# Sparse 3x3 convolution on one core: all input loads issued at the start, the first store held until the seventh load has landed

## The chip, the cores and the metric

The kernel runs on one core of one Trainium2 chip. The metric is the device time of one execution in microseconds (us), as the median of several runs. One core has five engines that run side by side and meet at semaphores: TensorE (PE, matmuls), VectorE (DVE), ScalarE (ACT), GpSimd (POOL) and SyncE (SP, which here only issues transfers). Transfers between the main memory (HBM) and the on-chip memory (SBUF) are carried by 16 DMA engines, which both transfer queues of this kernel share: SP's queue (q1 in the profile) and POOL's queue (q0).

## The reference

```python
def setup_inputs():
    batch, c_in, h, w, c_out, k = 16, 64, 64, 64, 128, 3
    ...
def reference(x, weight):
    x_pad = np.pad(x, ((0, 0), (0, 0), (pad, pad), (pad, pad)), mode='constant')
    ...
                        if weight[co, ci, kh, kw] != 0:
                            output[b, co] += weight[co, ci, kh, kw] * x_pad[b, ci, kh:kh+h, kw:kw+w]
```

It is a 3x3 convolution with padding 1 over 16 images of 64 channels and 64x64 points, to 128 output channels, all in float32. Nine tenths of the weights are zero, but not in a pattern that the kernel uses. The input x is 16.8 MB, the weight 0.3 MB, the output 33.6 MB.

## The kernel before

**Tiling.** Two images are worked on together as a pair, so there are eight pairs. A pair's input lies in one SBUF tile `xs[p]` of 128 partitions (image of the pair and channel) by 64x64 points in bf16, 8 KB per partition. The output of a pair is one tile of 128 output channels by 2 images by 64x64 points in float32, 32 KB per partition.

**Loads.** POOL issues the loads of x (`load`, L67 and L68), and each converts float32 to bf16 on the way, so that a load reads 2 MB and writes 1 MB. Pair 0 is split: its lower 32 rows come by POOL (L63), its upper 32 rows come unconverted by SP into `x_head` (L62) and are cast by VectorE and ScalarE (`cast_x`, L101). SP also loads the weight (L60). Then POOL issues pairs 1 to 3 and the first 24 rows of pair 4 at once (L72 to L77). The rest of the input is issued from inside the loop over pairs, each load behind POOL's last sum of a pair: the rest of pair 4 in pair 1, pair 5 in pair 2, pair 6 in pair 3, and the halves of pair 7 in pairs 4 and 5 (L196 to L199).

**Work of a pair.** A pair is cut into four blocks of 16 rows. All but one go through `twos` (L166): POOL adds each even row and the odd row below it into `s` (L169); TensorE multiplies `s` with the middle row of taps, ScalarE copies this shared product from PSUM into `pc` (L176), TensorE computes the even and the odd rows with differences of taps, and VectorE adds `pc` to them into the output tile (L183). The first block of pair 0 goes through `direct` (L159) without sums. TensorE's instructions stand in program order.

**Stores.** When a pair is complete, SP stores its 4.2 MB in one transfer (L207), and the last pair in two halves (L205). The output tiles come from a pool of three buffers: pair 3 writes where pair 0's output lay, so it waits until that store has landed. After pair 1's store SP issues five transfers of one number each into `spare` (L209 to L211). Each transfer of a queue signals on one of eight semaphores in turn, so these five shift which semaphore the later stores use.

**Order.** The schedule is the program's order on each engine (`manual_schedule`); the framework adds the semaphore waits from the memory that instructions read and write.

Of the kernel before, what the change touches and what calls it, by code (L numbers as in the profile page):

```python
# [8 lines left out]
FP32 = mybir.dt.float32  # L9
BF16 = mybir.dt.bfloat16  # L10
# [17 lines left out]
def kernel(  # L28
# [6 lines left out]
    nc = tc.nc  # L35

    B, C_IN, H, W = x.shape
    C_OUT, _, KH, KW = weight.shape
    assert (B, C_IN, H, W) == (16, 64, 64, 64) and (C_OUT, KH, KW) == (128, 3, 3)
    NP = B // 2  # L40
    HEAD = 32

    const_pool = ctx.enter_context(tc.tile_pool(name="const", bufs=1))
    x_pool = ctx.enter_context(tc.tile_pool(name="x", bufs=1))
    s_pool = ctx.enter_context(tc.tile_pool(name="s", bufs=3))
    p_pool = ctx.enter_context(tc.tile_pool(name="pc", bufs=4))
    o_pool = ctx.enter_context(tc.tile_pool(name="o", bufs=3))
    psum_pool = ctx.enter_context(
        tc.tile_pool(name="psum", bufs=8, space=bass.MemoryType.PSUM)
    )  # L50
# [4 lines left out]
    def pair(p):  # L55
        return x[2 * p : 2 * p + 2].rearrange("n i h w -> (n i) h w")

    xs = [x_pool.tile([128, H, W], BF16, name=f"x{p}") for p in range(NP)]
    w_sb = const_pool.tile([C_OUT, C_IN * KH * KW], FP32, name="w_sb")
    nc.sync.dma_start(out=w_sb, in_=weight.rearrange("o i kh kw -> o (i kh kw)"))  # L60
    x_head = const_pool.tile([128, HEAD, W], FP32, name="x_head")
    nc.sync.dma_start(out=x_head, in_=pair(0)[:, 0:HEAD, :])  # L62
    nc.gpsimd.dma_start(out=xs[0][:, HEAD:H, :], in_=pair(0)[:, HEAD:H, :])  # L63
    ident = const_pool.tile([128, 128], BF16, name="ident")
    make_identity(nc, ident)

    def load(p, a=0, b=H):  # L67
        nc.gpsimd.dma_start(out=xs[p][:, a:b, :], in_=pair(p)[:, a:b, :])  # L68

    EARLY, CUT = 4, 24  # L72

    LATER = {2: (5,), 3: (6,), 4: (7, 0, 32), 5: (7, 32, 64)}
    for p in range(1, EARLY):
        load(p)
    load(EARLY, 0, CUT)  # L77


    idle_rhs = const_pool.tile([128, 512], BF16, name="idle_rhs")  # L80
# [78 lines left out]
    def direct(p, o, r0, rows):  # L159
        ps = product(  # L160
            [(xs[p], G1, r0, 1), (xs[p], G0, r0 - 1, 1), (xs[p], G2, r0 + 1, 1)], rows
        )
        nc.scalar.copy(out=o[0][:, r0 : r0 + rows, :], in_=ps[0])  # L163
        nc.vector.tensor_copy(out=o[1][:, r0 : r0 + rows, :], in_=ps[1])  # L164

    def twos(p, o, r0):  # L166
        t0 = r0 // 2
        s = s_pool.tile([128, 8, W], BF16, name="s")
        nc.gpsimd.tensor_tensor(  # L169
            out=s, in0=xs[p][:, r0 : r0 + 16 : 2, :], in1=xs[p][:, r0 + 1 : r0 + 16 : 2, :], op=ADD  # L170
        )
        shared = product([(s, G1, 0, 1)], 8)
        pc = []
        for n in range(2):
            c = p_pool.tile([128, 8, W], FP32, name="pc")
            nc.scalar.copy(out=c, in_=shared[n])  # L176
            pc.append(c)
        even = [(xs[p], G21, r0 + 1, 2), (xs[p], G0, r0 - 1, 2)]
        odd = [(xs[p], G01, r0, 2), (xs[p], G2, r0 + 2, 2)]
        for first, terms in ((r0, even), (r0 + 1, odd)):  # L180
            ps = product(terms, 8)
            for n in range(2):
                nc.vector.tensor_tensor(  # L183
                    out=o[n][:, first : r0 + 16 : 2, :], in0=ps[n], in1=pc[n], op=ADD
                )

    for p in range(NP):
        both = o_pool.tile([C_OUT, 2, H, W], FP32, name="o")
        o = [both[:, n] for n in range(2)]
        into = out[2 * p : 2 * p + 2].rearrange("n o h w -> o n h w")  # L190
        last = p == NP - 1
        for blk in range(4):
            r0 = 16 * blk
            if BLOCKS[p][blk] == "T":
                twos(p, o, r0)
                if p == 1 and blk == 3:  # L196
                    load(EARLY, CUT, H)
                elif blk == 3 and p in LATER:
                    load(*LATER[p])  # L199
            else:  # L200
                for r, rows in ((r0, 8), (r0 + 8, 8)):
                    direct(p, o, r, rows)
            if last and blk % 2 == 1:
                rows = slice(r0 - 16, r0 + 16)
                nc.sync.dma_start(out=into[:, :, rows, :], in_=both[:, :, rows, :])  # L205
        if not last:
            nc.sync.dma_start(out=into, in_=both)  # L207
        if p == 1:
            spare = const_pool.tile([1, 5], FP32, name="spare")  # L209
            for k in range(5):  # L210
                nc.sync.dma_start(out=spare[:, k : k + 1], in_=weight[0:1, 0, 0, 0:1])  # L211


# [28 lines left out]
```

## Time and profile before

| What | Value |
|---|---|
| Median of 3 runs | 126.06 us (125.84 to 131.06) |
| Profiled execution, span from first to last instruction | 124.3 us |
| PE busy | 108.7 us (87%) |
| DVE, ACT, POOL busy | 82.5, 39.0, 41.7 us |
| q1 (SP's transfers) | 34.90 MB, 67.2% of 16 engines' span |
| q0 (POOL's loads, bytes as they land) | 7.86 MB, 30.7% |
| Issue of pair stores on SP, first and last | 23.0 us, 99.8 us |
| Issue of the two halves of pair 7 | 106.2 us, 112.6 us |
| A 4.2 MB store, issue to landing (median) | 19.8 us |

The profile is one execution taken by the hardware profiler. Its span leaves out what lies before the first and after the last instruction, so the runs' times are somewhat longer than the span. A share of busy time is an average over the span. In the page's slices, a digit is the busy share of one fortieth of the span in tenths. The rate of the DMA engines counts bytes at their destination.

### The profile page before, as it was taken

Reading aid. Unit: us, or ns where it says so; the run is one execution under the profiler, and the core shown is the slowest. Engines: PE = TensorE matmul, PEld = TensorE weight load, DVE = VectorE, ACT = ScalarE, POOL = GpSimd, SP = SyncE. Lnnn points to the kernel's source line nnn. Section 1 sums busy time; section 2 is a strip of 40 time slices with the busy share of each in tenths; the row PEclk is TensorE's granted clock in tenths of the full one; section 3 lists DMA queues with packets and bytes.
Section 4 is the critical chain, followed back from the end, with each engine's and each line's share of the span. In section 5 each row is a group of like instructions: output and inputs, shape, how many; then the busy total and the mean of one; then the engine's idle time right before and its main releaser. Section 6 shows DMA issues by size and latency. Waiting matters only on the chain.

```text
span 124.3 us, 2453 instructions
## 1 busy us (share of the span) xinstructions
PE 108.7 (87%) x989; PEld 57.2 (46%) x989; DVE 82.5 (66%) x135; ACT 39.0 (31%) x71; POOL 41.7 (34%) x47
## 2 busy tenths in 40 slices
PE   6959999999999999999999999999999999970000
PEld 2425555555555555555555555555555555530000
DVE  0353577877787778777877878887877787772000
ACT  4543333333333333333333333333333333330000
POOL 6409333533353335333443335333333320000000
PEclk9999999999999999999999999999999999997555
DMA  4999999999999999999999999999999999999991
GB/s 120 348 220 227 219 213 213 238 411 338 335 392 422 319 316 324 377 340 329 303 385 378 354 380 443 376 349 389 418 422 437 422 427 427 437 427 403 432 414 82
DMA packets 4198, 42.91 MB, mean 345 GB/s; under 512 B 347, under 2 KB 347, under 8 KB 1115
## 3 DMA queue, kind: packets, MB, share of 16 engines
q1 hardware_dynamic: 2746, 34.90, 67.2%
q0 software_dynamic: 1440, 7.86, 30.7%
q8 instruction: 7, 0.11, 0.3%
q14 instruction: 5, 0.03, 0.1%
HBM read 17.07 MB, written 33.55 MB: 407 GB/s over the span
## 4 chain that ended last, share of the span: by engine, by line
PE 82%; DMA 5%; DVE 1%; issue 1%; DVEq 0%; SPq 0%
PE ps L150 82%; DMA x_head<-in_x_dram 5%; DVE o L183 1%; DVEq L237 0%; DVE x L101 0%; SPq L60 0%; DVEq L183 0%
## 5 line engine op out<-in xcount | busy, mean ns | idle before, releaser
L183 DVE TENSOR_TENSOR o<-ps,pc 128x512 f32<-128x512 f32 x124 | 77.8, 686 | 22.1 <-PE ps L150 19.2
L150 PE MATMUL ps<-x,wT 64*128 64x504 bf16 (+3 forms) x780 | 88.8, 373 | 1.3 <-DVE x L101 1.3
L150 PEld LDWEIGHTS <-wT 64*128 64x128 bf16 x966 | 55.2, 94 | 49.5 <-issue 1.7
L169 POOL TENSOR_TENSOR s<-x 128x512 bf16<-128x512 bf16 x31 | 35.6, 1150 | 57.6 <-PE ps L150 41.1
L176 ACT COPY pc<-ps 128x512 f32<-128x512 f32 x62 | 33.3, 589 | 64.0 <-issue 61.8
L150 PE MATMUL ps<-s,wT 64*128 64x512 bf16 (+1 forms) x186 | 25.7, 377 | 0.0
L86 PE MATMUL ps<-idle_rhs 128*128 128x512 bf16 x14 | 4.8, 505 | 1.2 <-DVE idle_rhs L81 1.2
L68 POOL DMA_DIRECT2D x<-in_x_dram x9 | 5.0, 560 | 0.0
L86 PEld LDWEIGHTS <-idle_rhs 128*128 128x128 bf16 x14 | 1.5, 118 | 3.2 <-issue 1.4
L105 DVE CAST w_bf<-w_sb 128x192 bf16<-128x192 f32 (+1 forms) x4 | 1.1, 351 | 2.5 <-DMA w_sb<-in_weight_dram 2.5
L164 DVE COPY o<-ps 128x512 f32<-128x512 f32 x2 | 1.4, 692 | 2.0 <-PE ps L150 2.0
L101 DVE CAST x<-x_head 128x576 bf16<-128x576 f32 x1 | 0.5, 460 | 2.6 <-DMA x_head<-in_x_dram 2.6
L101 ACT CAST x<-x_head 128x576 bf16<-128x576 f32 (+1 forms) x2 | 1.5, 802 | 1.8 <-DMA x_head<-in_x_dram 1.8
L163 ACT COPY o<-ps 128x512 f32<-128x512 f32 x2 | 1.2, 586 | 2.4 <-PE ps L150 2.4
L105 ACT ACT_TABLE_LOAD x1 | 1.3, 1283 | 0.7 <-PEq L226 0.7
L105 ACT CAST w_bf<-w_sb 128x64 bf16<-128x64 f32 (+1 forms) x2 | 0.7, 416 | 1.6 <-DMA w_sb<-in_weight_dram 1.6
L115 DVE TENSOR_TENSOR wT<-ps,wT 128x384 bf16<-128x384 f32 x2 | 1.0, 548 | 0.0
L111 PEld LDWEIGHTS <-w_bf 128*128 128x128 bf16 x9 | 0.5, 97 | 1.0 <-DVE w_bf L105 1.0
L63 POOL DMA_DIRECT2D x<-in_x_dram x1 | 0.7, 693 | 0.8 <-POOLq L226 0.8
L111 PE MATMUL ps<-ident,w_bf 128*128 128x128 bf16 x9 | 0.9, 222 | 0.1
L81 DVE MEMSET idle_rhs<- 128x256 uint32 x1 | 0.3, 272 | 0.9 <-PEq L226 0.9
L126 DVE CAST wT<-ps 128x384 bf16<-128x384 f32 x1 | 0.6, 551 | 0.0
(8 smaller groups left out, 1.9 us busy)
## 6 DMA issues: line engine op xcount, KB each, us to landing
out_dram<-o SPq DMA_DIRECT2D x7, 4096.0 KB, 19.8
x<-in_x_dram POOLq DMA_DIRECT2D x5, 1024.0 KB, 16.8
out_dram<-o SPq DMA_DIRECT2D x2, 2048.0 KB
x<-in_x_dram POOLq DMA_DIRECT2D x3, 512.0 KB, 13.8
x_head<-in_x_dram SPq DMA_DIRECT2D x1, 1024.0 KB, 6.2
x<-in_x_dram POOLq DMA_DIRECT2D x1, 640.0 KB, 14.8
x<-in_x_dram POOLq DMA_DIRECT2D x1, 384.0 KB, 22.3
w_sb<-in_weight_dram SPq DMA_DIRECT2D x1, 288.0 KB
```

Source lines behind the costliest of these rows:

```text
L68: nc.gpsimd.dma_start(out=xs[p][:, a:b, :], in_=pair(p)[:, a:b, :])
L86: nc.tensor.matmul(idle_ps, idle_rhs[:, 0:128], idle_rhs, start=True, stop=True)
L101: copy(out=xs[0][:, a:b, :], in_=x_head[:, a:b, :])
L105: copy(out=w_bf4[:, g, a:b, :], in_=w_v[:, k : k + b - a, :])
L111: nc.tensor.matmul(wps[:, j, :], src, ident, start=True, stop=True)
L115: nc.vector.tensor_tensor(out=wT[:, g], in0=wps, in1=wT[:, G1], op=SUB)
L150: nc.tensor.matmul(ps[n][:, lo:hi, c_lo:c_hi], tap(g, kw, n), src[q, a:b:step, c_lo + kw - 1 : c_hi + kw - 1], start=(i == 0), stop=(i == ...
L163: nc.scalar.copy(out=o[0][:, r0 : r0 + rows, :], in_=ps[0])
L164: nc.vector.tensor_copy(out=o[1][:, r0 : r0 + rows, :], in_=ps[1])
L169: nc.gpsimd.tensor_tensor(out=s, in0=xs[p][:, r0 : r0 + 16 : 2, :], in1=xs[p][:, r0 + 1 : r0 + 16 : 2, :], op=ADD)
L176: nc.scalar.copy(out=c, in_=shared[n])
L183: nc.vector.tensor_tensor(out=o[n][:, first : r0 + 16 : 2, :], in0=ps[n], in1=pc[n], op=ADD)
```

## The change

- All of pairs 1 to 7 are loaded by POOL in one run ahead of everything else (`UP_FRONT = 8`); the loads inside the loop, and the splits of pairs 4 and 7, are gone.
- SP's first store, that of pair 0, gets an added wait: it is issued only when the load of pair 6 (`GATE = 6`, the seventh pair) has landed.
- There are four output tiles instead of three, used in turn. The fourth is one piece of memory, `shared_home`, with `x_head` and the input tiles of pairs 0, 1 and 2: pairs 3 and 7 write their output there.
- The five tiny transfers move from behind pair 1's store to the start, behind the loads of the weight and of `x_head`.

```diff
-    o_pool = ctx.enter_context(tc.tile_pool(name="o", bufs=3))
...
-    xs = [x_pool.tile([128, H, W], BF16, name=f"x{p}") for p in range(NP)]
+    shared_home = const_pool.tile([128, 4, H * W // 2], FP32, name="home")
+    x_head = shared_home[:, 0, :].rearrange("c (h w) -> c h w", w=W)
+    xs = [
+        shared_home[:, 1 + p, :].bitcast(BF16).rearrange("c (h w) -> c h w", w=W)
+        for p in range(3)
+    ]
+    xs += [x_pool.tile([128, H, W], BF16, name=f"x{p}") for p in range(3, NP)]
+    outs = [const_pool.tile([C_OUT, 2, H, W], FP32, name=f"o{k}") for k in range(3)]
+    outs.append(shared_home.rearrange("o (n r) (h w) -> o n (r h) w", n=2, w=W))
...
-    EARLY, CUT = 4, 24
-
-    LATER = {2: (5,), 3: (6,), 4: (7, 0, 32), 5: (7, 32, 64)}
-    for p in range(1, EARLY):
-        load(p)
-    load(EARLY, 0, CUT)
+    UP_FRONT, GATE = 8, 6
+    landed = {p: load(p) for p in range(1, UP_FRONT)}
+    spare = const_pool.tile([1, 5], FP32, name="spare")
+    for k in range(5):
+        nc.sync.dma_start(out=spare[:, k : k + 1], in_=weight[0:1, 0, 0, 0:1])
...
-        both = o_pool.tile([C_OUT, 2, H, W], FP32, name="o")
+        both = outs[p % 4]
...
-                if p == 1 and blk == 3:
-                    load(EARLY, CUT, H)
-                elif blk == 3 and p in LATER:
-                    load(*LATER[p])
...
-        if not last:
-            nc.sync.dma_start(out=into, in_=both)
-        if p == 1:
-            spare = const_pool.tile([1, 5], FP32, name="spare")
-            for k in range(5):
-                nc.sync.dma_start(out=spare[:, k : k + 1], in_=weight[0:1, 0, 0, 0:1])
+        if not halves:
+            store = nc.sync.dma_start(out=into, in_=both)
+            if first:
+                tc.add_manual_dep(
+                    store.ins,
+                    landed[GATE].ins.name,
+                    mybir.DependencyInfo(
+                        mybir.DependencyClass.Sync, mybir.DependencyReason.DATA
+                    ),
+                    reason="stores begin when the loads are nearly through",
+                )
+                first = False
```

More of the change, by code (lines that the diff above doesn't have):

```diff
@@ L56, in pair @@
         return x[2 * p : 2 * p + 2].rearrange("n i h w -> (n i) h w")
-    xs = [x_pool.tile([128, H, W], BF16, name=f"x{p}") for p in range(NP)]
+    shared_home = const_pool.tile([128, 4, H * W // 2], FP32, name="home")
[7 more added lines that the diff above has]
+    outs.append(shared_home.rearrange("o (n r) (h w) -> o n (r h) w", n=2, w=W))
     w_sb = const_pool.tile([C_OUT, C_IN * KH * KW], FP32, name="w_sb")
     nc.sync.dma_start(out=w_sb, in_=weight.rearrange("o i kh kw -> o (i kh kw)"))
-    x_head = const_pool.tile([128, HEAD, W], FP32, name="x_head")
     nc.sync.dma_start(out=x_head, in_=pair(0)[:, 0:HEAD, :])
@@ L67, in load @@
     def load(p, a=0, b=H):
-        nc.gpsimd.dma_start(out=xs[p][:, a:b, :], in_=pair(p)[:, a:b, :])
-    EARLY, CUT = 4, 24
-    LATER = {2: (5,), 3: (6,), 4: (7, 0, 32), 5: (7, 32, 64)}
-    for p in range(1, EARLY):
-        load(p)
-    load(EARLY, 0, CUT)
+        return nc.gpsimd.dma_start(out=xs[p][:, a:b, :], in_=pair(p)[:, a:b, :])
+    UP_FRONT, GATE = 8, 6
[3 more added lines that the diff above has]
+        nc.sync.dma_start(out=spare[:, k : k + 1], in_=weight[0:1, 0, 0, 0:1])
     idle_rhs = const_pool.tile([128, 512], BF16, name="idle_rhs")
@@ L185, in twos @@
                 )
+    first = True
     for p in range(NP):
-        both = o_pool.tile([C_OUT, 2, H, W], FP32, name="o")
+        both = outs[p % 4]
         o = [both[:, n] for n in range(2)]
         into = out[2 * p : 2 * p + 2].rearrange("n o h w -> o n h w")
-        last = p == NP - 1
+        halves = p == NP - 1
         for blk in range(4):
@@ L202 @@
                     direct(p, o, r, rows)
-            if last and blk % 2 == 1:
+            if halves and blk % 2 == 1:
                 rows = slice(r0 - 16, r0 + 16)
                 nc.sync.dma_start(out=into[:, :, rows, :], in_=both[:, :, rows, :])
-        if not last:
-            nc.sync.dma_start(out=into, in_=both)
-        if p == 1:
-            spare = const_pool.tile([1, 5], FP32, name="spare")
-            for k in range(5):
-                nc.sync.dma_start(out=spare[:, k : k + 1], in_=weight[0:1, 0, 0, 0:1])
+        if not halves:
[10 more added lines that the diff above has]
+                first = False
 _INS = ['x', 'weight']
```

## Prediction

> **What bounds the kernel now.** I read the page's slices first, because engines and transfers stand side by side there.
>
> ```profile
> PE   6959999999999999999999999999999999970000
> DMA  4999999999999999999999999999999999999991
> GB/s 120 348 220 227 219 213 213 238 411 338 335 392 422 319 316 324 377 340 329 303 385 378 354 380 443 376 349 389 418 422 437 422 427 427 437 427 403 432 414 82
> ```
>
> Two rows are full. TensorE works from 7.95 us to about 111 and then stops; the DMA engines work from the second slice to the last. So the end is a matter of transfers, while TensorE sets when each store may start. The rate row looks as if the loads ran at half speed (220 against 430), but it counts the bytes that arrive: x is float32 in memory and bf16 when it lands, so a load moves two bytes for each byte counted. The views of the DMA queues over three stretches allow a fair count: loads alone, loads and stores mixed, stores alone.
>
> ```profile
> DMA packets 464, 3.22 MB, mean 215 GB/s; under 512 B 58, under 2 KB 58, under 8 KB 81
> q0 software_dynamic: 463, 3.21, 102.6%
> ...
> DMA packets 2103, 23.42 MB, mean 360 GB/s; under 512 B 174, under 2 KB 174, under 8 KB 668
> q1 hardware_dynamic: 1244, 19.17, 70.4%
> q0 software_dynamic: 851, 4.15, 31.1%
> ...
> DMA packets 1007, 12.82 MB, mean 427 GB/s; under 512 B 64, under 2 KB 64, under 8 KB 65
> q1 hardware_dynamic: 1003, 12.80, 100.2%
> ```
>
> The stretches are 8 to 23 us, 23 to 88 and 88 to 118. Counting loads (q0) double and adding 0.02 to 0.1 MB of instruction fetch, the rates are 6.44 MB / 15 us = 429 GB/s for loads alone, 27.57 MB / 65 us = 424 for the mixture, 12.83 MB / 30 us = 427.7 for stores alone. The mixture is slower by about one per cent and no more. The same count gives 8.78 MB before 23 us and 1.59 MB after 118, together 50.77 MB.
>
> The windows show how it ends (the last two numbers of a row are the share of 16 DMA engines and GB/s), and the timeline when SP issues the stores of pairs 0 and 1, the five tiny transfers, and the last two stores:
>
> ```profile
> 118.00:120.00 2.00, 0.00 (x0) 0.00 (x0) 0.00 (x0) 0.00 (x0) 0.00 (x0) 0.50 0.99 422
> 120.00:122.00 2.00, 0.00 (x0) 0.00 (x0) 0.00 (x0) 0.00 (x0) 0.00 (x0) 0.50 0.78 332
> 122.00:124.30 2.30, 0.00 (x0) 0.00 (x0) 0.00 (x0) 0.00 (x0) 0.00 (x0) 0.50 0.09 36
> ```
>
> ```profile
> 23.03 13.13 SPq L207 DMA_DIRECT2D out_dram<-o  x2
> 36.22 4.93 SPq L211 DMA_DIRECT2D spare<-in_weight_dram  x5
> 48.58 51.60 SPq L207 DMA_DIRECT2D out_dram<-o  x5
> 106.16 6.82 SPq L205 DMA_DIRECT2D out_dram<-o  x2
> ```
>
> The last store is issued at 112.6, and its 2.1 MB would take 4.9 us on a free queue; data ends near 123, so a backlog stood before it. The 16 engines do not stop together: some stop just before 121 us, the last at 123. The chain of waits ends at 112.6 and puts 82% on TensorE: it does not follow the last transfers, and I do not use it for the end.
>
> **The change, part by part.**
>
> *Bytes.* Eight loads instead of ten carry the same bytes; stores and weights are the same. Whatever the change gains in transfers, it gains by rate.
>
> *Order.* After 23 us the kernel before moves 27.57 MB mixed, in 65 us. Now the 8.30 MB of loads in it go alone: 8.30 / 0.429 = 19.35 us, to 42.35 us. The 19.17 MB of stores go alone at 427.7 GB/s, 44.8 us, and 0.1 MB of instruction fetch takes 0.25. Together 64.4 us against 65.0: a gain of 0.6 us. From below, if order is worth nothing, 0. From above, the largest rate of one slice (443) is one slice's scatter, so I do not take it; 433 for all mixed bytes, the best 5 us window of stores alone (95 to 100 us), would give 1.3 us.
>
> A rule speaks against this gain. The Trainium skill, page "HBM Reference", section "Specifications (TRN2)", says that a core streaming alone gets about 425 GB/s and is held by its 16 DMA engines. By that rule the order of reads and writes is worth nothing; 50.77 MB at 425 would be an estimated 119.5 us in either order. The 424 of the mixture agrees; that the two unmixed stretches stand 0.9 to 1.2% higher is what I set against it.
>
> *The wait of the first store.* Through pair 6 the loads have 8.30 - 2.10 = 6.20 MB left at 23 us: 14.45 us, to 37.5. A load lands later than its mean data, since the slowest engine decides: pair 3's, issued at 3.53, landed at 24.17, where the byte count puts its data at 22.8, so 1.4 us. The store is issued at 38.9, and its first data moves 1.3 us later (as in the trace before: issue 23.03, first store packet 24.31), at 40.2. The load of pair 7 covers the engines until 42.35, so the wait costs nothing, with 2.1 us of cover. Without that cover each us would be an idle us of all engines. Behind the waiting store on SP stands only the store of pair 1, ready at 35.8, which must queue behind pair 0's in any case. No engine waits for SP.
>
> *Can the stores be supplied?* TensorE's pace is unchanged, so pair 6's store comes at 99.8 us, its data at 101.1. In the kernel before, 14.42 MB are left at 88 us (12.83 and 1.59), of which pair 6 and 7 are 8.39; the other 6.03 last 14.1 us, to 102.1. So there the queue never empties, by 1.0 us. With 0.6 us gained it empties at 101.5, still after 101.1. This caps the gain: from 101.1, 8.39 MB at 427.7 end at 120.7 at the earliest.
>
> *Buffers.* Pair 4 writes over pair 0's buffer, at 61.95 us before. Pair 0's store ends its data at 42.35 + 9.8 = 52.2 and lands some 2 us later: 8 us of cover, and later pairs have more (9.8 us per store against 12.8 us per pair of compute). With three buffers pair 3 would have met it at 48.6, hence the fourth; it lies over x_head and pairs 0 to 2, read for the last time before pair 3's sums, so TensorE's own order has already met that wait. A few first-time semaphore waits on VectorE, bounded by its 0.58 us pauses per block, cost nothing; without that idle time (VectorE is busy 66%) some tenths once.
>
> *POOL's issues.* Three more loads stand ahead of POOL's first sum, at 0.54 us each (four took 2.15): issuing ends at 4.61 + 1.6 = 6.2 us, the sum starts at 9.04. Five later issues (0.57 us each) go out of POOL's idle time. Nothing on the path, with 2.8 us of cover.
>
> *SP's tiny transfers.* Five issues, 4.93 us, move from 36 us to about 1.6 to 6.5 us, behind the weight and x_head, before a store that now waits until 38.9. Nothing; no byte of weight.
>
> *Tail.* Engines end up to 2 us apart, and the latest decides. If unmixed traffic evens them out, up to 1 us is gained; if not, nothing. At the pure loads, landing lags are already there, so I take 0.
>
> *Sum.* Span 124.3 - 0.6 = 123.7. The median of the runs, 126.06, is 1.7 above this execution's span, which stays: **125.4 us**.
>
> **Rivals.**
>
> *Order is worth nothing* (126.1). For it: the three rates lie within 1.2%, and single slices scatter by more. Against it: each stretch is 15 us or longer.
>
> *The engines even out as well* (about 124.4). The gain of 0.6 and 1.0 from the tail; at the cap, data ending at 120.7 with all engines together, span 122.1 and time 123.8. For it: shares of 0.78 and 0.09 in the last stretches. Against it: nothing shows that mixing sets them apart, and pure stores from 88 to 118 do not bring them together. Only near this cap does the time approach the 2% that about what a measurement of this kernel can tell from no change.
>
> *POOL is held at the issue of loads* (slower). Before, at most five loads were outstanding; now eight. If there is room for six, the seventh issue waits for the first landing (9.04 us, harmless), the eighth for pair 1's at 13.9; POOL is free at 14.5, its sum is ready at 15.6, where TensorE wants it at 11.76. TensorE is 3.9 us late, pair 6's store moves data at 105.0 instead of 102.1: 126.1 + 2.9 = 129.0. With room for five the eighth waits for pair 2's landing at 19.3, the sum comes at 21.0, 9.3 us late: 134.4. With room for seven or eight nothing happens: that is the point from which it decides. Against it: all five issues in the trace take 0.52 to 0.69 us with no growth.
>
> *The wait opens too late* (about 127). If load 6 lands 2 us later against its data than pair 3's did, plus the store's 1.3 us, the cover of 2.1 us is used up, and as the later slack is only 1.0 us, the rest reaches the end: a landing lag of 4.5 us would cost 1.0. Loads at the 412 GB/s of single slices would add 0.8 us.
>
> **How the numbers follow.** Forecast 0.42 (124.6 to 126.0); order worth nothing 0.17; engines even out 0.18, of which 0.11 below the 2% line at 123.5; POOL held 0.12, all beyond the line at 128.6; late opening 0.11, of which 0.04 beyond it. Faster 0.11, slower 0.16, same 0.73. The range goes from 123.6, a little below the cap, to 127.8, which takes in the late opening and leaves out POOL's case.
>
> **What would show it.** In the profile after: the rate row at about 215 to 220 until slice 13 or 14 (42 us) and about 427 from there without a dip; TensorE full from 8 to 111 us; SP's first store issued near 39; POOL's first sum still near 9.0. A dip near 40 us means the late opening, one near 101 the cap; a TensorE gap near 12 us means POOL was held. Any rate in the pure stretches other than 424 to 432 makes the main term wrong.

## Result, and the profile after

| | Before | After |
|---|---|---|
| Median of 5 runs | 126.06 us | 127.17 us (127.03 to 127.33) |
| Ratio of the runs, 95% interval | 1 | 1.0081 (1.0056 to 1.0106) |
| Span of the profiled execution | 124.3 us | 125.3 us |

The change makes the kernel slower by 0.8%. That is less than 2%, and the time lies inside the range that was given; but the forecast was a gain of 0.6 us, the medians show a loss of 1.1 us, and the whole interval lies above 1. Some executions run several per cent slower as a whole (one of the five before took 131.06 us); the ratios and intervals here and below leave such executions out.

These are the slices of the page after (TensorE, DMA engines, rate), then two rows of its DMA queues: loads alone (8 to 40 us) and stores alone (45 to 112 us).

```profile
PE   6999999999999999999999999999999999940000
DMA  4999999999999999999999999999999999999970
GB/s 133 336 220 225 212 215 217 212 220 217 215 212 220 298 416 429 434 434 426 424 424 434 424 429 434 429 416 419 434 439 434 432 413 424 434 405 429 421 301 13
```

```profile
DMA packets 961, 6.92 MB, mean 216 GB/s; under 512 B 114, under 2 KB 114, under 8 KB 122
q0 software_dynamic: 956, 6.89, 103.2%
...
DMA packets 1872, 28.60 MB, mean 427 GB/s; under 512 B 107, under 2 KB 107, under 8 KB 107
q1 hardware_dynamic: 1864, 28.51, 100.0%
```

The rate row looks as the prediction drew it: 210 to 225 to slice 13, then 405 to 439, with no hole at the hand-over near 40 us and none near 101 us. With loads counted double, the loads alone run at (2 x 6.89 + 0.03) / 32 us = 431.6 GB/s and the stores alone at 28.60 / 67 us = 426.9; 429 and 427.7 were forecast. TensorE is full from 8 to 110 us as before.

The SP timeline after shows the wait (start, length, line, transfer); the row below it is from the waits of SP:

```profile
1.66 1.63 SPq L80 DMA_DIRECT2D spare<-in_weight_dram  x5
39.23 9.57 SPq L207 DMA_DIRECT2D out_dram<-o  x3
...
106.01 6.82 SPq L205 DMA_DIRECT2D out_dram<-home  x2
```

```profile
SPq L207 <- DMA x<-in_x_dram: 35.9, 1, 35.9
```

The first store goes out at 39.23 us (38.9 was forecast), the last half again at 112.5. So far the steps of the prediction hold, and still the end is later. The windows at the end show where (the last two numbers are DMA share and GB/s):

```profile
118.00:120.00 2.00, 0.00 (x0) 0.00 (x0) 0.00 (x0) 0.00 (x0) 0.00 (x0) 0.50 1.02 430
120.00:122.00 2.00, 0.00 (x0) 0.00 (x0) 0.00 (x0) 0.00 (x0) 0.00 (x0) 0.50 0.56 238
122.00:125.20 3.20, 0.00 (x0) 0.00 (x0) 0.00 (x0) 0.00 (x0) 0.00 (x0) 0.50 0.04 18
```

Between 120 and 122 us only 0.56 of the engines' time is used; before it was 0.78. Most engines end earlier than before, and a remnant of 0.04 over 3.2 us goes on. Sixteen engines times 0.04 times 3.2 us are 2.0 us of one engine's time, so this is little more than one engine working alone. The single packets of the trace tell more. Each of the 16 engines closes a transfer with a 4-byte packet of its own, and the 16 of the last store say when each engine ended:

```
engine ends (us)    first    median   15th     last
before              120.96   121.99   122.89   122.98
after               120.44   121.55   122.39   123.90
```

The median engine ends 0.44 us earlier: this is most of the forecast gain (0.6). The 15th ends 0.50 us earlier. The last one ends 0.92 us later and sets the span (125.26 - 124.34 = 0.92). Followed back packet by packet, this last engine takes 634 to 662 ns for its store packets of 16 KB from 66 to 112 us, where the others take 611.

The closing packets also tell when it fell behind. From one pair's store to the next, an engine that nothing disturbs takes 9.72 us in the kernel after. The engine that ends last can be followed from store to store:

```
closing packets of a store, us     1st    2nd    3rd    4th    5th    6th    7th
the engine that ends last          52.4   62.7   73.0   83.3   93.6  104.0  114.1
its place among the 16             10     12     12     15     16     16     16
the last engine                    54.3   64.0   73.7   83.4   93.6  104.0  114.1
```

It takes 10.30 to 10.32 us five times over, and 10.15 us for the step in which TensorE ends: 0.6 us lost in each store, evenly. It began as the tenth of the 16, 1.9 us ahead of the last one, and ends 1.5 us behind the 15th. No step holds a jump of about 1 us, as an instruction fetch would make on one engine. With the last engine of each kernel left out, the end would be the 15th's: 122.39 us after, 122.89 before, a gain.

### The profile page after: what moved, and what is told of

It reads as the page before. It is cut to its first block, busy times and chain, and to the rows that moved or that the text cites. A ratio compares the mean times of both kernels' runs of the same rounds, so it can differ in the third digit from the quotient of the medians.

```text
span 125.3 us, 2485 instructions
## 1 busy us (share of the span) xinstructions
PE 109.9 (88%) x989; PEld 49.7 (40%) x989; DVE 82.4 (66%) x135; ACT 38.9 (31%) x71; POOL 40.8 (33%) x45
## 4 chain that ended last, share of the span: by engine, by line
PE 87%; DVE 1%; issue 1%; DVEq 1%
PE ps L153 81%; PE ps L89 4%; DVE home L186 1%; PE ps L114 1%; DVEq L243 0%; DVE idle_rhs L84 0%; DVEq L186 0%
## 5 line engine op out<-in xcount | busy, mean ns | idle before, releaser
L153 PEld LDWEIGHTS <-wT 64*128 64x128 bf16 x966 | 47.1, 94 | 56.2 <-ACT home L104 0.4
L186 DVE TENSOR_TENSOR o<-ps,pc 128x512 f32<-128x512 f32 x92 | 57.7, 686 | 16.6 <-PE ps L153 14.8
L153 PE MATMUL ps<-x,wT 64*128 64x504 bf16 (+2 forms) x480 | 54.4, 373 | 0.0
L172 POOL TENSOR_TENSOR s<-x 128x512 bf16<-128x512 bf16 x20 | 23.1, 1155 | 40.9 <-PE ps L153 31.0
L153 PE MATMUL ps<-home,wT 64*128 64x504 bf16 (+3 forms) x300 | 33.9, 373 | 0.0
L186 DVE TENSOR_TENSOR home<-ps,pc 128x512 f32<-128x512 f32 x32 | 20.1, 686 | 5.5 <-PE ps L153 4.2
L172 POOL TENSOR_TENSOR s<-home 128x512 bf16<-128x512 bf16 x11 | 12.6, 1154 | 17.4 <-PE ps L153 10.9
L74 POOL DMA_DIRECT2D x<-in_x_dram x5 | 2.7, 565 | 0.0
L104 ACT CAST home<-home 128x576 bf16<-128x576 f32 (+1 forms) x2 | 1.5, 802 | 1.0 <-DMA home<-in_x_dram 1.0
L74 POOL DMA_DIRECT2D home<-in_x_dram x2 | 1.1, 548 | 0.0
```

Of the source, the lines that this page charges most:

```text
L74: return nc.gpsimd.dma_start(out=xs[p][:, a:b, :], in_=pair(p)[:, a:b, :])
L104: copy(out=xs[0][:, a:b, :], in_=x_head[:, a:b, :])
L153: nc.tensor.matmul(ps[n][:, lo:hi, c_lo:c_hi], tap(g, kw, n), src[q, a:b:step, c_lo + kw - 1 : c_hi + kw - 1], start=(i == 0), stop=(i == ...
L172: nc.gpsimd.tensor_tensor(out=s, in0=xs[p][:, r0 : r0 + 16 : 2, :], in1=xs[p][:, r0 + 1 : r0 + 16 : 2, :], op=ADD)
L186: nc.vector.tensor_tensor(out=o[n][:, first : r0 + 16 : 2, :], in0=ps[n], in1=pc[n], op=ADD)
```

## Experiments

The theory from here on: **one DMA engine falls behind while stores run alone**. Counted over the stretch in which stores run alone before TensorE ends, packets of 16 KB that took 627 to 720 ns, and what they took beyond the others, added up:

```
kernel        stores alone from   slow packets   excess, us   median end   last end
before             89 us               36           1.26        121.99      122.98
late_loads         88                  36           1.30        121.75      122.60
mix_longer        103                  10           0.39        122.29      122.87
no_gate            62                  76           2.84        122.14      123.78
after              45                 110           4.12        121.55      123.90
third_after        45                  42           1.30        120.87      122.19
```

In the kernel after, some eight of these fall in 5 us, and 5 us hold just 7.7 packets of 650 ns: one engine's worth. The excess of 4.12 us is not the lag at the end, because the slow engine began ahead of those that were last then.

**no_gate: the wait taken away.**

```diff
-            store = nc.sync.dma_start(out=into, in_=both)
-            if first:
-                tc.add_manual_dep(store.ins, landed[GATE].ins.name, ...)
+            nc.sync.dma_start(out=into, in_=both)
```

> The changed kernel without the added wait of the first store: all loads still up front, four output buffers, tiny transfers at the start. Theory 'one slow DMA engine': in the profile after, exactly one engine's worth of 16 KB store packets (8 in 5 us) takes about 650 ns instead of 611 while stores run alone (42 to 112 us), which delays that engine by about 0.06 us for each us of stores alone. Without the wait the loads mix with stores from 24 to about 61 us, so stores run alone for some 50 us instead of 70: about 1.1 us less delay, 0.4 us given back by the slower mixture: about 126.5. Rival 'the wait itself': the hand-over near 40 us leaves some engines behind, and that is the whole loss: 126.1 or less. Rival 'the fourth buffer or the moved tiny transfers': 127.2, no change.

Measured: 127.19 us, the median of the ten runs that the ratio uses; ratio 1.0102 (1.0061 to 1.0142). The wait is not the loss. My 126.5 was missed as well; the 127.2 of the last rival was met, and the next run tests that rival. The table shows why the time stayed: the slow engine's excess fell by 1.3 us as expected, but the median engine ended 0.6 us later than in the changed kernel. The loss shows at the hand-over, now near 25 us, where load packets took up to 1262 ns instead of 625. Counted at their source, the bytes move at 381 GB/s from 24 to 32 us, which loses 0.9 us on all engines, but at 426 from 32 to 60 us, still mixed.

**late_loads: the loads of before, with the four buffers and the early tiny transfers.**

```diff
-    UP_FRONT, GATE = 8, 6
-    landed = {p: load(p) for p in range(1, UP_FRONT)}
+    EARLY, CUT = 4, 24
+    LATER = {2: (5,), 3: (6,), 4: (7, 0, 32), 5: (7, 32, 64)}
+    for p in range(1, EARLY):
+        load(p)
+    load(EARLY, 0, CUT)
...
+                if p == 1 and blk == 3:
+                    load(EARLY, CUT, H)
+                elif blk == 3 and p in LATER:
+                    load(*LATER[p])
```

The added wait is gone here too.

> The loads of the kernel before (inside the loop) and no added wait, but the four output buffers, the shared memory and the tiny transfers at the start, as in the changed kernel. Theory 'one slow DMA engine' and rival 'the wait itself': 126.1, as before. Rival 'the fourth buffer or the moved tiny transfers': 127.2.

Measured: 126.34 us, ratio 1.0012 (0.9983 to 1.0041). The fourth buffer, its place over the inputs and the moved tiny transfers cost nothing clear of the interval, at most 0.5 us. What remains is when the loads run.

**relief: less work for one engine.**

```diff
-                nc.sync.dma_start(out=into[:, :, rows, :], in_=both[:, :, rows, :])
+                for c in (slice(0, 120), slice(120, 128)) if blk == 1 else (slice(0, 128),):
+                    nc.sync.dma_start(out=into[c, :, rows, :], in_=both[c, :, rows, :])
```

> The changed kernel, except that the store of the first half of pair 7 goes in two transfers, channels 0 to 119 and 120 to 127. 120 channels split evenly over 15 DMA engines, so one engine should get none of it (4.9 us less work), and the 8 channels left should lie on 8 other engines (0.6 us more). Theory 'one slow DMA engine', if the slow one is the one left out: the end is set by the next engines (122.4 us plus up to 0.6 in the profile after, against 123.9): 125.7 to 126.3. If it is another engine: 127.2 to 127.8. Rival 'the wait itself' (engines left behind at the hand-over, not always the same one): about 127.2.

Measured: 131.65 us, the median of the three runs that the ratio uses; ratio 1.0468 (1.0397 to 1.0538). All the times expected were missed. It tells nothing on the theory, because the transfer of 120 channels brings a loss of its own. The windows of this kernel (DMA share, GB/s last) are from an execution of 134.84 us, so the loss in them is some 3 us larger than in that median:

```profile
112.00:118.00 6.00, 0.00 (x0) 0.00 (x0) 0.20 (x1) 0.00 (x0) 0.00 (x0) 0.79 0.98 266
118.00:124.00 6.00, 0.00 (x0) 0.00 (x0) 0.00 (x0) 0.00 (x0) 0.00 (x0) 0.50 0.93 295
```

The engines are busy, but at 266 to 295 GB/s instead of 427: packets of 8 KB took 309 ns in the kernel after, here many take more, up to 2231.

The next kernels whose names begin with `stores_` leave out the convolution and keep little but the stores. Each was run once, and they serve only to read its trace.

**stores_only: the stores with nothing beside them.**

```diff
-    (all loads of x beyond one row, all compute)
+    for k in range(4):
+        nc.vector.memset(outs[k], 0.0)
+    for p in range(NP):
+        into = out[2 * p : 2 * p + 2].rearrange("n o h w -> o n h w")
+        nc.sync.dma_start(out=into, in_=outs[p % 4])
```

> Only the stores: no loads of x, no matmuls, no POOL or ScalarE work; four buffers are filled with zeros by VectorE and stored eight times, as whole pairs. Theory 'one slow DMA engine': still one engine's worth of 16 KB packets (112 to 128 of 2048) at 640 to 660 ns, the others at 611 to 620, so the slow one ends 4 to 5 us after the others. Rival: the slow packets come from other traffic on the chip's memory (VectorE, matmuls, POOL's sums) and are gone here, all engines ending within 1 us.

Measured: span 90.4 us; from 45 us on, when VectorE's fills are over, 2 slow packets of 1142, and all engines end every store within 0.2 us of each other. (During the fills, packets up to 665 ns appear, but on all engines alike.) So the engine is not slow by itself, and my expectation fell: stores alone are not enough. Something that runs beside them makes it slow. The next runs add one thing at a time.

**stores_pe and stores_vec: one kind of work beside the stores.**

```diff
+    for i in range(900):
+        q = slice(64 * (i % 2), 64 * (i % 2) + 64)
+        nc.tensor.matmul(pss[i % 2], rhs[q, 0:128], rhs[q], start=True, stop=True)
```

> Only the stores, as in the run with stores alone (where all engines stayed within 0.2 us of each other), and 900 matmuls of zeros on TensorE beside them; nothing else runs. If TensorE's activity (its records, or its instruction fetches) is what makes one DMA engine slow: one engine's worth of packets at 640 to 660 ns, 8 in 5 us, and the engines drift apart by 0.06 us per us, 4 us at the end. If not: no drift beyond 1 us per instruction fetch on one engine.

```diff
+    for i in range(110):
+        nc.vector.tensor_tensor(out=to_v, in0=ps_v, in1=pc_v, op=ADD)
+    for i in range(125):
+        nc.scalar.copy(out=to_a, in_=ps_a)
+    for i in range(65):
+        nc.gpsimd.tensor_tensor(out=to_p, in0=sb[:, 0], in1=sb[:, 1], op=ADD)
```

> Only the stores, and beside them VectorE adds, ScalarE copies and POOL sums in the shapes of the kernel, without pause; no matmuls. If the reads and writes of these engines in the on-chip memory, or their instructions, make one DMA engine slow: one engine's worth of packets at 640 to 660 ns and a drift of 0.06 us per us. If TensorE's activity does it: engines within 0.5 us.

Measured from 45 us on: with matmuls 69 slow packets, 637 ns on average, excess 1.55 us; with the other three engines, each busy 93% or more, 6 slow packets, 0.2 us. With TensorE at work there is a slow engine, with the other three at work there is none. The matmul run also shows a second effect: behind an instruction fetch at 48.65 us (16 KB, 931 ns on one engine) three store packets of that engine took 858 to 1005 ns, and it ended the store 1.9 us after the others. Three such fetches before the end left three engines 1.6 to 1.9 us late at the end, beside the slow one, 1.4 us late. TensorE's 900 matmuls started only at 35.7 us, after the fills, so the drift was shorter than expected.

**stores_pe_f32: TensorE as busy, with fewer instructions.**

```diff
-    rhs = const_pool.tile([128, 512], BF16, name="rhs")
+    rhs = const_pool.tile([128, 512], FP32, name="rhs")
...
-    for i in range(900):
+    for i in range(225):
```

> The stores with matmuls beside them, but 225 float32 matmuls instead of 900 bf16 ones, each about four times as long: TensorE as busy, with a quarter of the instructions. With 900 one engine's packets took some 25 ns longer (7 to 8 in 5 us above 627 ns). If the number of instructions causes it: no engine above 627 ns, or 6 to 8 ns longer, and one instruction fetch at most. If TensorE's reading of the on-chip memory causes it: the same 7 to 8 packets in 5 us.

The windows of the bf16 run and of the float32 run from 45 to 88 us (TensorE busy and count, weight loads and count):

```profile
45.00:88.00 43.00, 43.00 (x402) 19.27 (x400) 0.00 (x0) 0.00 (x0) 1.00 1.01 426
```

```profile
45.00:88.00 43.00, 43.00 (x204) 19.11 (x202) 0.00 (x0) 0.00 (x0) 1.00 1.01 427
```

A float32 matmul shows as two records, so it is half the instructions, not a quarter. TensorE is busy all 43 us in both. Slow packets fall from 69 to 10, excess from 1.55 to 0.20 us, and the ten no longer follow one another on one engine. So it is not TensorE's busy time. It may be the number of its instructions; but the edit lowers two more things, which this run does not separate from it: counted from the program, a quarter of the matmuls with elements twice as large read half the bytes and write a quarter of the results in about the same time.

**stores_skew: two engines put out of step.**

```diff
+        if p == 2:
+            two = const_pool.tile([2, 3, H * W], FP32, name="two")
+            for k in range(3):
+                nc.sync.dma_start(out=two[:, k], in_=x[k, 0:2].rearrange("i h w -> i (h w)"))
```

> Only the stores, but after the third store two DMA engines get 48 KB more each (three small loads on two partitions), 1.9 us of work, so that they run out of step with the others from then on. If an engine is slow because it is out of step with the others: these two show packets of 640 to 660 ns after 40 us and their lag grows by 0.06 us per us, to 4 or 5 us. If being out of step is harmless: the lag stays at about 1.9 us to the end.

Measured: the two engines fall 4.0 us behind through these loads, and 39 us later they are 3.65 us behind (1.9 was expected for both). No slow packet. Being late by itself does not make an engine slow; with TensorE at work beside it this was not tested.

**mix_longer: loads spread over a longer time, in the kernel before.**

```diff
-    LATER = {2: (5,), 3: (6,), 4: (7, 0, 32), 5: (7, 32, 64)}
+    LATER = {
+        (1, 3): (4, CUT, 64), (2, 3): (5, 0, 48), (3, 1): (5, 48, 64), (3, 3): (6, 0, 16),
+        (4, 1): (6, 16, 32), (4, 3): (6, 32, 48), (5, 1): (6, 48, 64), (5, 3): (7, 0, 16),
+        (6, 1): (7, 16, 32), (6, 3): (7, 32, 48), (7, 1): (7, 48, 64),
+    }
```

> The kernel before, with the loads inside its loop cut into smaller pieces (mostly 16 rows) and issued later, so that loads go on beside the stores until about 102 us instead of 89. Theory 'one DMA engine falls behind while stores run alone': some 10 us of stores alone before TensorE ends instead of 24, so about 16 slow packets of 16 KB instead of 33 and about 0.7 us less delay on that engine; as the next engines end only 0.1 to 0.4 us before it, the time is 125.6 to 126.0. Rival 'mixing loads and stores costs one per cent, and what is lost in the changed kernel is something else that loading early brings': 14 us more of mixture cost 0.1 to 0.2 us: 126.2. A store that comes too late for an empty queue (the margins are 1 to 2 us) would show as a dip in the rate and cost up to 1 us.

Measured: 126.30 us against 125.78 of the kernel before on the same chip, ratio 1.0035 (1.0001 to 1.0069). The excess fell from 1.26 to 0.39 us, as expected, but the median engine ended 0.3 us later, and the gain I forecast did not come: the 126.2 of the rival is nearer. One reading is that the kernel before stands near a balance, where more mixture slows all engines and less mixture slows one. It rests on medians 0.3 us apart in one execution each, and in no_gate the mixture behind the hand-over ran at 426 GB/s, so it is not shown.

**third_after and third_before: a third of the matmuls.**

```diff
-KW_ORDER = (1, 0, 2)
+KW_ORDER = (1,)
```

> The kernel before with only the middle column of taps: a third of the matmuls of the convolution, all transfers and all work of the other engines kept. TensorE no longer sets the pace of the stores; the end is a matter of transfers. Theory 'TensorE's activity makes one DMA engine slow while stores run alone, and each of its instruction fetches holds up one engine': two fetches instead of seven, few slow packets: 124.5 to 125.5. Rival 'the slow engine has nothing to do with TensorE': 126 or a little less, 33 slow packets in some 24 us of stores alone.

> The changed kernel with only the middle column of taps (a third of the matmuls). Theory 'TensorE's activity makes one DMA engine slow': the slow packets are rarer or milder, the slow engine ends less than 1 us after the others, and the 0.5 us that the unmixed transfers save on the undisturbed engines reach the end: 124.0 to 124.8, and 0.3 to 0.8 us faster than the kernel before with the same third. Rival 'the slow engine has nothing to do with TensorE, it comes with stores alone': still some 110 slow packets of 640 to 660 ns, and slower than the kernel before with the same third by 0.8 to 1.5 us.

Measured: the changed kernel 125.56 us, ratio to the kernel before 0.9958 (0.9938 to 0.9977); the kernel before with the same cut 126.32 us, 1.0018 (0.9984 to 1.0052). The changed kernel gains 1.6 us (127.17 to 125.56) with the same transfers in the same order. Its windows at the end:

```profile
118.00:120.00 2.00, 0.00 (x0) 0.00 (x0) 0.00 (x0) 0.00 (x0) 0.00 (x0) 0.50 1.02 430
120.00:122.00 2.00, 0.00 (x0) 0.00 (x0) 0.00 (x0) 0.00 (x0) 0.00 (x0) 0.50 0.38 160
122.00:125.00 3.00, 0.00 (x0) 0.00 (x0) 0.00 (x0) 0.00 (x0) 0.00 (x0) 0.50 0.00 0
```

The straggler beyond 122 us is all but gone. The first engine ends only 0.25 us earlier than in the changed kernel (120.19 against 120.44), the last one 1.7 us earlier. From 95 us on, when TensorE has ended, not one slow packet appears, though stores still run alone. Instruction fetches fell from seven to two as well, so the cut takes away both of TensorE's effects; but the last engine of the changed kernel is the slow one, whose steps from store to store hold no fetch, and the next ended at 122.39.

The comparison with third_before, which I had meant as the sharper test, is spoiled. Its rate row shows a loss that the others lack:

```profile
GB/s 117 350 230 213 218 213 213 137 310 350 353 325 318 318 326 326 324 387 389 363 347 426 421 392 378 343 442 431 426 437 426 421 434 426 442 413 418 431 429 87
```

The eighth slice is at 137 where loads alone give 213. Between 22 and 26 us, where the first store meets a load that is cut into small packets, the bytes counted at their source come at 282 GB/s instead of 430: 0.6 MB, 1.4 us. So 126.32 misses the 124.5 to 125.5 that I expected, and that third_after is the faster of the two by 0.76 us is not shown to be the effect of the order alone.

**markers: which engine is it?**

```diff
-    for k in range(5):
-        nc.sync.dma_start(out=spare[:, k : k + 1], in_=weight[0:1, 0, 0, 0:1])
...
+            if p == 4:
+                for k, n in enumerate((2, 4, 6, 8, 12, 14)):
+                    nc.sync.dma_start(out=marks[0:n, k : k + 1], in_=weight[0:n, 0, 0, 0:1])
```

> The changed kernel; the five tiny transfers at the start are replaced by six of 2, 4, 6, 8, 12 and 14 numbers behind the store of pair 4. A transfer of n partitions goes to n engines, so each engine carries its own count of these tiny packets. Which count stands in the row of slow packets shows which engine it is: by the order of the engines 0 for the last two, 6 for the first two. Time as the changed kernel, 127.2. If not always the same engine is slow, the slow packets before and after pair 4's store lie in rows with different counts.

Measured: 128.37 us in one run; 108 slow packets, excess 4.11 us, the last engine at 124.53. The engine that ends the store of pair 4 last, at 94.3 us, and goes on with packets of 644 to 669 ns, carries nine tiny packets there: its own closing packet and two for each of four transfers. Four of the six belong, in the order of the engines counted from 0, to number 4 or 5. Before that point its packets could not be told from others' in this run. In the kernel after, the closing packets follow one slow engine from 52 us to the end; whether it is the same one in every execution was not shown.

The Trainium skill, page "DMA: Bandwidth & Descriptors", says in "Why a DMA increments its semaphore by 16 and not by 1" that such a transfer on n partitions uses the lowest n engines; the numbering rests on it. In "Latency and other measured facts" it says that engines 7 and 15 are usually the slower ones in traces. Here one engine is slower too, but by the markers it is 4 or 5, and only under the conditions above.

## Why the prediction was wrong

- **Bounds and rates: right in size, the reason half open.** The end is set by transfers; unmixed loads and stores run at 431.6 and 426.9 GB/s, and the median engine gains 0.44 us of the 0.6. That speaks for the row and against the rule of the Trainium skill's page "HBM Reference" that I had set beside it, by which order would be worth nothing. But the 424 GB/s of the mixture was an average: in the kernel before, the first 9 us behind the hand-over (23 to 32 us) ran at 414 and the rest, to 88 us, at 426. About 0.3 of the forecast 0.6 us lay in those 9 us. How much of the 0.44 is the order, and how much is what happens where stores first meet loads, is not shown.
- **The wait: right.** Issue at 39.23 us, no hole; taking it away (no_gate) does not help.
- **Supply, buffers, tiny transfers: right.** Pair 6's store is issued at 99.66 us, the rate has no dip, no engine waits for a store's landing, and late_loads shows no cost of the rest of the change.
- **POOL's issues: right.** They end at 6.2 us, as worked out, and its first sum starts at 8.48. That rival is out.
- **The tail: wrong.** This is the step that failed. I wrote that engines end up to 2 us apart, that unmixed traffic may even them out by up to 1 us, and took 0. I had looked at the mean of 16 engines and bounded the tail on one side only: "up to 1 us is gained; if not, nothing". The sentence that nothing shows the mixture to set the engines apart was a misreading too: in the trace before, the landing signals of a store's 16 engines lie 3.3 us apart for the stores that landed at 71 and 83 us, and 1.9 to 2.2 from 94 us on. So the spread changes with the traffic, and had to be bounded above as well. In fact the last engine went from 0.99 us behind the median to 2.35, a loss of 1.36 us: 1.36 - 0.44 = 0.92 us, the difference of the spans.
- **What takes the gain.** While stores run alone and TensorE issues its instructions, one of the 16 DMA engines takes about 650 ns for a packet instead of 611. Before, this lasted from 89 to 112 us (excess 1.26 us); loading everything first stretches it to 45 to 112 us (4.12 us). In the mixed stretches it does not stand out: before, 1103 of 1170 store packets between 24 and 88 us took 611 to 624 ns, and in no_gate only one of 490 between 24 and 62 us took 627 to 720. The rival *the engines even out* had its sign reversed; *order is worth nothing* gave 126.1, nearer to the 127.17 than my forecast, for a reason that is not the true one.

Shown: that the last engine of the kernel after loses about 0.6 us in every store while TensorE works, and that of the 16 ends, put in order, only the last is later than before; that such an engine appears beside the stores with TensorE at work (stores_pe) and not without (stores_only, stores_vec); and that with a third of the matmuls the changed kernel nearly loses its straggler. Argued only: that it is the number of TensorE's instructions, and not what they read and write. Open: why TensorE's work slows one DMA engine, whether the profiler's own records have a part in it, and why loads, alone or mixed in, do not suffer.

No version tried beats both kernels with all taps.

## What to carry to other kernels

A transfer ends with its slowest engine. Where transfers set the end, read when each DMA engine finishes and not only the mean rate: a reordering can speed up fifteen engines and still lose by the sixteenth. And bound a spread from both sides: what may even out may also grow with the length of the stretch that makes it.

## What the runs showed of the hardware that was not expected

- With dense instructions on TensorE, one DMA engine's 16 KB store packets took about 650 ns instead of 611 (the kernel after; 637 instead of 615 in stores_pe); with VectorE, ScalarE and POOL busy and TensorE idle (stores_vec), there was no such engine.
- An instruction fetch of 16 KB takes 0.88 to 1.0 us of one DMA engine, and beside stores alone slowed the next packets too, 1.9 us in all (stores_pe).
- A store of 120 of 128 channels, followed by the other 8, ran at 266 to 295 GB/s instead of 427 (relief).
- Where stores first met loads, all engines lost time: 381 GB/s instead of 426 for 8 us in no_gate, 282 instead of 430 for 4 us in third_before.
- In stores_skew, two engines that were late stayed late: 4.0 us behind, and 3.65 us behind after 39 us of equal work.
